# The first two right operands of the up projection's first set, made in a task of the output projection

## Chip, cores and metric

The kernel runs on one core of one Trainium2 chip. The metric is the device time of one execution in microseconds; the time before is the median of three runs. One more execution was taken by the hardware profiler, and all views below come from it.

## What is computed

One decoder layer on 2048 tokens of width 1024: two groups of gated linear attention between two norms, then an MLP with squared ReLU. Cut to what matters here:

```python
def reference(x, w_in, ..., w_out, pre_mix_norm, post_mix_norm, pre_mlp_norm, post_mlp_norm, w_up, w_down):
    h = x
    mix = hybrid_mixer(rmsnorm(h, pre_mix_norm), w_in, ..., w_out)   # (2048, 1024); ends with "@ w_out"
    h = h + rmsnorm(mix, post_mix_norm)
    u = rmsnorm(h, pre_mlp_norm) @ w_up                              # (1024, 4096)
    m = jnp.square(jax.nn.relu(u)) @ w_down                          # (4096, 1024)
    return h + rmsnorm(m, post_mlp_norm)
```

All inputs and the output are float32.

## The kernel before

**Products of split operands.** Each float32 operand is split in a high part (an ACT copy, rounded to float32r) and a low part (the difference, on DVE or POOL). A product is three matmuls: high by high, high by low, low by high. In `up`'s `product` these are L1064 (high parts), L1065 (left's low part) and L1066 (right's low part).

**Stages.** The mixer runs over four blocks of 512 tokens. Each ends with `out_proj`, which multiplies by w_out in two halves of columns. For each 128 tokens (a row of tokens, in what follows) a `residual` task then scales the result (L867), adds the input (L868), squares it for the next norm (L870 on ACT), stores it to out (L873), scales it again (L874), transposes it on TensorE (L880) and stores it to a scratch tensor. After the mixer comes `up`, then `down`.

**Up as a seven-product scheme.** Each 2 x 2 block product is done with seven products of sums instead of eight. The left operands come from activations: sums that `combine` has stored in h_operands. The right ones come from w_up: for one *set* (256 columns of w_up) four blocks b11, b12, b21, b22, from which `right` makes seven operands, number 0 being b11 itself, number 5 being t2 = b22 - t1 with t1 = b12 - b11, and so on (t4 = b21 - t2). Products go in the order 0, 5, 1, 6, 4, 3, 2; 0 and 1 collect in PSUM bank X, 5, 6 and 3 in Y, 4 and 2 in Z. There are 16 sets for each half of the tokens.

**What overlaps.** For the last block, `out_proj` asks SP to load the first set's raw weights in two stage tiles (`st`, 128 x 1024), long ahead, and starts the task `first_left`. It loads the eight quarters of left operands 0 and 5 from h_operands in `ct` tiles (128 x 512, 15 slots), and splits them (`left`, L934; `parts`, whose ACT copy is L951; `tt`, L948 on DVE or L945 on POOL). The set's right operands are made by `right` in tiles of a pool that lies where the mixer's weights were, so only when the output projection has read those. `up` first runs the products of sets 0 and 1 that can begin within seven slots, among the last `residual` steps (L874 to L884).

**What sets the order.** Tasks are Python generators. `step` advances each by one yield; that gives the order in which instructions are recorded. A scheduler of the framework then orders them, engine by engine, by its own estimate of times, and each engine runs its list in order. SP issues nearly all DMAs, in order too: one that waits holds those behind it. `tt` chooses DVE or POOL by the load it has given each so far.

The second copy of the layer (`exact`) is for inputs outside the range of the fast one and does not run here.

Of the kernel before, what the change touches and what calls it, by code (L numbers as in the profile page):

```python
# [7 lines left out]
F32 = mybir.dt.float32  # L8
F32R = mybir.dt.float32r
I32 = mybir.dt.int32  # L10
AF = mybir.ActivationFunctionType
ALU = mybir.AluOpType
# [4 lines left out]
P = 128  # L17
# [49 lines left out]
class Weights:  # L67
# [17 lines left out]
    def part(self):  # L85
        y = self.layer
        return y.wp.tile([P, 2, WS], F32R, tag="w", name=y.name("w"), bufs=self.LIVE)
# [59 lines left out]
class Layer:  # L147
# [631 lines left out]
    def out_proj(self, b):  # L779
        nc = self.nc  # L780
        mix = [self.t([P, D], "wide") for _ in range(NCH)]
        ss = [self.t([P, 2], "ssm", bufs=8) for _ in range(NCH)]
        heads = [2 * u + h for u in UNITS for h in range(2)]

        def part(z, t, w, ks):
            for i in ks:
                a = tuple(s[:, t * P:(t + 1) * P] for s in self.oT[heads[i]])
                self.mm3(z, a, w[i], i, KT)

        def evac(z, t, half):  # L790
            nc.scalar.activation(mix[t][:, half * 512:half * 512 + 512], z, AF.Copy)
            junk = self.ct()
            nc.scalar.activation(junk, z, AF.Square, accum_out=ss[t][:, half:half + 1])

        if b + 1 < NBLK:
            self.hn[b + 1] = []
            nxt = self.prepare(b + 1)
        else:
            self.ops = {(0, i): [] for i in self.ORDER}
            st = [self.stage(), self.stage()]  # L800
            for x in st:
                self.after(x, self.rs[b][0])
            self.first = [self.up_raw(0, half, x) for half, x in enumerate(st)]
            nxt = self.first_left()
        w, zs = [], []
        for t in range(NCH):
            self.w.pump(2)
            zs.append(self.zp())
            for i in range(6):
                if t == 0:  # L810
                    w.append(self.w.take())
                part(zs[t], t, w, (i,))
                if i % 3 == 2:
                    self.step()
        while len(self.oT) < 8:
            self.step()
        if not self.exact:
            self.spawn(nxt)
        w += [self.w.take(), self.w.take()]
        for t in range(NCH):  # L820
            part(zs[t], t, w, (6, 7))
            if t == NCH - 1:
                self.w.free(KT)
            evac(zs[t], t, 0)
            self.w.pump(2)
            if t % 2:
                self.step()
        w = []
        for t in range(NCH):
            z = self.zp()  # L830
            for i in range(KT):
                if i % 4 == 0:
                    self.w.pump(2)
                if t == 0:
                    w.append(self.w.take())
                part(z, t, w, (i,))
                if t == NCH - 1:
                    self.w.free()
                if i == 3:
                    self.step()  # L840
            evac(z, t, 1)
            self.step()
        for t in range(NCH):
            self.spawn(self.residual(b * TB + t * P, mix[t], ss[t], t))
        if self.exact:
            self.spawn(nxt)
            self.drain()
        elif b + 1 < NBLK:
            self.drain(nxt)
    def first_left(self):  # L850

        for i in self.ORDER[:2]:
            yield from self.left(0, i, self.ct, self.ops[0, i], self.aslots)

# [118 lines left out]
    def up(self):  # L973
# [4 lines left out]
        with ExitStack() as ctx:  # L978
# [3 lines left out]
            def new(tag, n, dt=F32, width=512):  # L982
                sb = upa if tag in ("ev", "a") else self.upw
                return sb.tile([P, width], dt, tag=tag, name=self.name(tag), bufs=n)
# [26 lines left out]
            def right(n):  # L1011

                g = n % NG
                raw = []
                for half in range(2):
                    r = self.up_raw(g, half, new("wr", 4, F32, 1024)) if n else self.first[half]
                    raw += [r[:, :, :P], r[:, :, P:]]
                b11, b12, b21, b22 = raw
                w = sets[n] = {}
                part = lambda z: self.parts(  # L1020
                    *(new("w", 12, F32R).rearrange("p (k n) -> p k n", k=4) for _ in range(2)), z)

                def t():
                    return new("t", 5).rearrange("p (k n) -> p k n", k=4)

                yield
                w[0] = part(b11)
                t1 = t()
                self.tt(t1, b12, b11, ALU.subtract)
                yield  # L1030
                t2 = t()
                self.tt(t2, b22, t1, ALU.subtract)
                w[5] = part(t2)
                yield
                w[1] = part(b21)
                t4 = t()
                self.tt(t4, b21, t2, ALU.subtract)
                yield
                t3 = t()
                self.tt(t3, b22, b12, ALU.subtract)  # L1040
                w[6] = part(t3)
                yield
                w[4] = part(t1)
                yield
                w[3] = part(t4)
                yield
                w[2] = part(b22)
                yield
# [98 lines left out]
            def do(n, what):  # L1147
                if isinstance(what, int):
                    left(n // NG, what)
                    return  # L1150
                if (n, what) not in run:
                    run[n, what] = {
                        "product": lambda: product(n), "right": lambda: right(n),
                        "combine": lambda: self.combine(n // NG + 1, quarters),
                        "down": lambda: self.first_down(new),
                    }[what]()
                next(run[n, what], None)
# [402 lines left out]
```

## Time and profile before

| | |
|---|---|
| three runs | 2253.69 to 2256.93 us, median 2256.26 |
| the profiled execution | 2258.14 us, span of its instructions 2256.3 us |
| TensorE busy | 2201.9 us (98%) |
| DVE, ACT, POOL busy | 1416.8, 1090.1, 643.5 us |
| granted TensorE clock | 0.994 |
| first matmul of up | 982.41 us from the span's start |

PE is TensorE's matmuls, PEld its weight loads, DVE the vector engine, ACT the scalar engine, POOL GpSimd, SP the queue that issues DMAs. In a timeline a row is start, duration, engine, line, operation, what is written <- what is read, and in brackets how long the engine stood before it and who ended the wait. [...] In the table of stretches each engine has its busy time in the stretch. Line numbers in all profile rows are those of the kernel before.

### The profile page before, as it was taken

The numbers are of one execution on the slowest core, as the hardware profiler recorded it, in microseconds if no ns is written. First come the engines' busy times: TensorE is split into PE (matmuls) and PEld (weight loads), VectorE is DVE, ScalarE is ACT, GpSimd is POOL, SyncE is SP. The second block draws the span as 40 slices with busy tenths as digits, with TensorE's granted clock in tenths as the row PEclk, the third lists the DMA queues.
The fourth block names the chain that finished last, engine by engine and source line by source line (L and its number), as shares of the span: only waits on it lengthen the run. The fifth ranks groups of instructions, "written<-read, shape, count | busy, mean of one in ns | idle before, by whom it ended". The sixth has DMA issues, their size and how long they took to land.

```text
span 2256.3 us, 30683 instructions
## 1 busy us (share of the span) xinstructions
PE 2201.9 (98%) x10922; PEld 1830.0 (81%) x10922; DVE 1416.8 (63%) x2273; ACT 1090.1 (48%) x2104; POOL 643.5 (29%) x444
## 2 busy tenths in 40 slices
PE   8999999999999999999999999999999999999996
PEld 7788888888888878876888878888778878888885
DVE  7765566444643475377765686656536876777687
ACT  6664565335543554366555665555542332233255
POOL 4444301010100220035522333223312333232344
PEclk9999999999999999999999999999999999999998
DMA  7766974477536974478744564443534343443357
GB/s 241 259 236 247 330 252 149 159 254 266 184 130 237 352 263 159 144 249 293 279 155 153 183 223 160 154 151 139 196 107 137 125 131 103 131 140 119 115 148 134
DMA packets 249810, 428.02 MB, mean 190 GB/s; under 512 B 19872, under 2 KB 93872, under 8 KB 249648
## 3 DMA queue, kind: packets, MB, share of 16 engines
q1 hardware_dynamic: 245520, 418.10, 54.0%
q0 software_dynamic: 3552, 6.82, 1.9%
q8 instruction: 88, 1.44, 0.3%
q10 hardware_dynamic: 576, 1.05, 0.1%
q14 instruction: 74, 0.61, 0.1%
HBM read 289.44 MB, written 136.45 MB: 189 GB/s over the span
## 4 chain that ended last, share of the span: by engine, by line
PE 49%; DMA 2%; DVE 1%; ACT 1%; issue 1%; POOL 1%; SPq 0%; DVEq 0%; ACTq 0%; POOLq 0%
PE Y_f L1365 4%; PE Y_f L1366 3%; PE Y_f L1367 3%; PE Y_f L1064 3%; PE Y_f L1065 3%; PE Y_f L1066 3%; PE X_f L1365 2%; PE X_f L1367 2%; PE Z_f L1064 2%; PE Z_f L1065 2%; PE X_f L1366 2%; PE Z_f L1066 2%; PE Z_f L1365 2%; PE Z_f L1367 2%; PE X_f L1066 2%; PE Z_f L1366 2%
## 5 line engine op out<-in xcount | busy, mean ns | idle before, releaser
L301 PE MATMUL zp_f<-w_f,act_f 128*128 128x512 f32 (+2 forms) x896 | 328.2, 367 | 4.1 <-DVE ct_f L319 3.3
L302 PE MATMUL zp_f<-w_f,act_f 128*128 128x512 f32 (+2 forms) x896 | 324.5, 362 | 0.0
L303 PE MATMUL zp_f<-w_f,act_f 128*128 128x512 f32 (+2 forms) x896 | 323.1, 363 | 0.0
L951 ACT ACTIVATE u_f<-raw_f 128x1024 fp32r<-128x1024 f32 x107 | 113.9, 1064 | 333.2 <-PE Y_f L1366 220.9
L310 POOL TENSOR_TENSOR rs_f<-ms_f,c_neghalf 128x1 f32<-128x1 f32 (+1 forms) x80 | 65.2, 821 | 651.2 <-DVE ms_f L308 645.6
L945 POOL TENSOR_TENSOR u_f<-raw_f,u_f 128x1024 fp32r<-128x1024 f32 x49 | 119.9, 2448 | 306.6 <-ACT u_f L951 305.6
L301 PEld LDWEIGHTS zp_f<-w_f,act_f 128*128 128x128 f32 x896 | 168.5, 188 | 31.0 <-DVE ct_f L319 3.7
L303 PEld LDWEIGHTS zp_f<-w_f,act_f 128*128 128x128 f32 x896 | 168.8, 188 | 24.6 <-issue 0.5
L302 PEld LDWEIGHTS zp_f<-w_f,act_f 128*128 128x128 f32 x896 | 168.9, 188 | 24.0 <-issue 0.5
L301 PE MATMUL zp_f<-act_f,w_f 128*128 128x512 f32 x384 | 151.9, 399 | 8.1 <-ACT act_f L294 8.1
L302 PE MATMUL zp_f<-act_f,w_f 128*128 128x512 f32 x384 | 152.3, 397 | 0.1
L303 PE MATMUL zp_f<-act_f,w_f 128*128 128x512 f32 x384 | 151.9, 396 | 0.0
L1320 DVE TENSOR_TENSOR acc_f<-acc_f,Y_f 128x1024 f32<-128x1024 f32 (+1 forms) x91 | 107.5, 1182 | 65.5 <-PE Y_f L1367 64.4
L1365 PE MATMUL Y_f<-act_f,u_f 128*128 128x512 f32 x368 | 143.7, 394 | 4.2 <-ACT u_f L951 2.2
L1366 PE MATMUL Y_f<-act_f,u_f 128*128 128x512 f32 x368 | 144.4, 392 | 0.0
L1367 PE MATMUL Y_f<-act_f,u_f 128*128 128x512 f32 x368 | 143.9, 393 | 0.1
L951 ACT ACTIVATE w_f<-t_f 128x512 fp32r<-128x512 f32 x128 | 80.2, 630 | 111.3 <-PE Y_f L1065 56.3
L292 POOL TENSOR_TENSOR w_f<-wr_f,w_f 128x512 fp32r<-128x512 f32 (+1 forms) x76 | 104.5, 1385 | 102.3 <-ACT w_f L291 98.4
L1066 PE MATMUL X_f<-act_f,w_f 128*128 128x512 f32 x256 | 100.8, 394 | 5.4 <-DVE w_f L948 3.8
L1084 DVE TENSOR_TENSOR ev_f<-Y_f,p_f 128x512 f32<-128x512 f32 x94 | 64.6, 687 | 63.1 <-PE Y_f L1066 63.1
L948 DVE TENSOR_TENSOR w_f<-t_f,w_f 128x512 fp32r<-128x512 f32 x96 | 80.2, 836 | 36.7 <-ACT w_f L951 36.7
L1320 DVE TENSOR_TENSOR acc_f<-acc_f,Z_f 128x1024 f32<-128x1024 f32 (+1 forms) x62 | 73.2, 1181 | 47.6 <-PE Z_f L1367 47.4
(302 smaller groups left out, 5773.7 us busy)
## 6 DMA issues: line engine op xcount, KB each, us to landing
w_f<-w_split SPq DMA_DIRECT2D x188, 512.0 KB, 6.2
raw_f<-u_operands SPq DMA_DIRECT2D x224, 256.0 KB, 3.1
u_operands<-ev_f SPq DMA_DIRECT2D x223, 256.0 KB, 2.1
w_split<-w_f SPq DMA_DIRECT2D x64, 512.0 KB, 5.2
wr_f<-in_w_up SPq DMA_DIRECT2D x62, 512.0 KB, 3.5
wide_f<-in_x SPq DMA_DIRECT2D x32, 512.0 KB, 7.0
wr_f<-in_w_mix SPq DMA_DIRECT2D x64, 256.0 KB, 5.0
wr_f<-in_w_down SPq DMA_DIRECT2D x28, 512.0 KB, 4.4
```

Source lines behind the costliest of these rows:

```text
L301: mm(out, a[0], b[0], start=i == 0, stop=False)
L302: mm(out, a[0], b[1], start=False, stop=False)
L303: mm(out, a[1], b[0], start=False, stop=i == n - 1)
L945: nc.gpsimd.tensor_tensor(out, a, b, op)
L951: self.nc.scalar.activation(hi, raw, AF.Copy)
L1064: mm(z, whi[:, k, :], hi, start=first and k == 0, stop=False, skip_group_check=more)
L1065: mm(z, whi[:, k, :], lo, start=False, stop=False, skip_group_check=more)
L1066: mm(z, wlo[:, k, :], hi, start=False, stop=end, skip_group_check=more)
L1320: nc.vector.tensor_add(a[:, cols], a[:, cols], z[:, cols])
L1365: mm(zx, hi[:, k, tok], whi, start=not loaded and k == 0, stop=False, skip_group_check=loaded)
L1366: mm(zx, hi[:, k, tok], wlo, start=False, stop=False, skip_group_check=loaded)
L1367: mm(zx, lo[:, k, tok], whi, start=False, stop=k == 1, skip_group_check=loaded)
```

## The change

`out_proj` of the last block keeps the two stage tiles in `self.raw`. `first_left`, before its loads and splits of the left operands, now makes the first set's right operand 0 (split of b11), the differences t1 and t2, and right operand 5 (split of t2), with a yield after each. They go in six `ct` tiles of the mixer instead of the `w` and `t` tiles of up's pool. `right` takes them from there for set 0 and makes them as before for all others. No load, split or matmul is added or left out.

```diff
@@ out_proj @@
             self.first = [self.up_raw(0, half, x) for half, x in enumerate(st)]
+            self.raw = st
             nxt = self.first_left()
@@ first_left @@
+        b11, b12, _, b22 = (r.rearrange("p (k n) -> p k n", k=4)[:, :, h * P:h * P + P]
+                            for r in self.raw for h in range(2))
+
+        def new(dt=F32):
+            return self.ct(dt).rearrange("p (k n) -> p k n", k=4)
+
+        w0 = self.parts(new(F32R), new(F32R), b11)
+        yield
+        t1 = new()
+        self.tt(t1, b12, b11, ALU.subtract)
+        yield
+        t2 = new()
+        self.tt(t2, b22, t1, ALU.subtract)
+        yield
+        self.first_right = w0, self.parts(new(F32R), new(F32R), t2), t1, t2
+        yield
         for i in self.ORDER[:2]:
             yield from self.left(0, i, self.ct, self.ops[0, i], self.aslots)
@@ right, in up @@
                 yield
-                w[0] = part(b11)
-                t1 = t()
-                self.tt(t1, b12, b11, ALU.subtract)
+                if n:
+                    w[0] = part(b11)
+                    t1 = t()
+                    self.tt(t1, b12, b11, ALU.subtract)
                 yield
-                t2 = t()
-                self.tt(t2, b22, t1, ALU.subtract)
-                w[5] = part(t2)
+                if n:
+                    t2 = t()
+                    self.tt(t2, b22, t1, ALU.subtract)
+                    w[5] = part(t2)
+                else:
+                    w[0], w[5], t1, t2 = self.first_right
                 yield
                 w[1] = part(b21)
```

What this does to the order shows at three places. In the changed kernel the lines behind the added ones have other numbers: L934 is L952, L873 is L891, L862 is L880, L962 is L980; L867, L868, L874 are L885, L886, L892; L880 is L898; L945, L948, L951 are L963, L966, L969; L1064 to L1066 are L1086 to L1088.

SP, around the stores of the first two rows of tokens to out, before (three of the eight ct loads stand above these rows):

```order
L934 DMA ct_f_9413<-h_operands 128x512
L934 DMA ct_f_9431<-h_operands 128x512
L873 DMA out<-wide_f_9164 128x1024
L934 DMA ct_f_9451<-h_operands 128x512
L934 DMA ct_f_9469<-h_operands 128x512
L934 DMA ct_f_9489<-h_operands 128x512
L873 DMA out<-wide_f_9165 128x1024
L962 DMA wr_f_9555<-in_w_up 128x1024
L962 DMA wr_f_9557<-in_w_up 128x1024
```

And now, with all eight:

```order
L952 DMA ct_f_9423<-h_operands 128x512
L891 DMA out<-wide_f_9164 128x1024
L952 DMA ct_f_9443<-h_operands 128x512
L952 DMA ct_f_9461<-h_operands 128x512
L952 DMA ct_f_9481<-h_operands 128x512
L952 DMA ct_f_9499<-h_operands 128x512
L891 DMA out<-wide_f_9165 128x1024
L980 DMA wr_f_9542<-in_w_up 128x1024
L952 DMA ct_f_9519<-h_operands 128x512
L980 DMA wr_f_9544<-in_w_up 128x1024
L952 DMA ct_f_9549<-h_operands 128x512
L952 DMA ct_f_9568<-h_operands 128x512
```

Four quarters of left operands have moved behind the first store, three behind the second, and the last three stand among the loads of set 1's raw weights (wr).

DVE, from the second row's scaling on (act is a split left operand, t and w those of right operands, ms, ss and rs belong to the norms), before:

```order
L874 TENSOR_SCALAR wide_f_9620<-wide_f_9165,rs_f_9663 128x1024
L867 SCALAR_TENSOR_TENSOR wide_f_9166<-wide_f_9166,rs_f_9726,post_f_656 128x1024
L948 TENSOR_TENSOR t_f_9541<-st_f_9172 128x512
L868 TENSOR_TENSOR wide_f_9166<-wide_f_9166,wide_f_9720 128x1024
L948 TENSOR_TENSOR t_f_9543<-st_f_9173,t_f_9541 128x512
L864 TENSOR_TENSOR ss_f_9791<-ssm_f_9171 128x1
L948 TENSOR_TENSOR t_f_9567<-st_f_9173,st_f_9172 128x512
L948 TENSOR_TENSOR t_f_9585<-wr_f_9555 128x512
L308 TENSOR_SCALAR ms_f_9748<-ss_f_9746 128x1
L308 TENSOR_SCALAR ms_f_9793<-ss_f_9791 128x1
L948 TENSOR_TENSOR w_f_9546<-t_f_9543,w_f_9545 128x512
```

And now, from the first of its subtractions behind that scaling on:

```order
L966 TENSOR_TENSOR t_f_9540<-st_f_9173,ct_f_9389 128x512
L966 TENSOR_TENSOR t_f_9559<-st_f_9173,st_f_9172 128x512
L886 TENSOR_TENSOR wide_f_9166<-wide_f_9166,wide_f_9720 128x1024
L966 TENSOR_TENSOR w_f_9537<-st_f_9173,w_f_9536 128x512
L966 TENSOR_TENSOR t_f_9582<-wr_f_9542 128x512
L882 TENSOR_TENSOR ss_f_9791<-ssm_f_9171 128x1
L966 TENSOR_TENSOR t_f_9628<-wr_f_9544,t_f_9582 128x512
L308 TENSOR_SCALAR ms_f_9748<-ss_f_9746 128x1
L308 TENSOR_SCALAR ms_f_9793<-ss_f_9791 128x1
L966 TENSOR_TENSOR t_f_9696<-wr_f_9544,t_f_9628 128x512
L966 TENSOR_TENSOR t_f_9752<-wr_f_9544,wr_f_9542 128x512
L966 TENSOR_TENSOR act_f_9546<-ct_f_9519,act_f_9546 128x512
```

The differences t1 and t2 and the low part of right operand 5 are gone from here, t4 (t_f_9540, on POOL before) is new here, and low parts of left operands follow, which before all stood above.

TensorE, product 5 of set 0 (bank Y_f_9698), before:

```order
L1064 MATMUL Y_f_9698<-act_f_9448,w_f_9545 128x512
L1065 MATMUL Y_f_9698<-act_f_9448,w_f_9545 128x512
L1066 MATMUL Y_f_9698<-act_f_9448,w_f_9546 128x512
L1064 MATMUL Y_f_9698<-act_f_9466,w_f_9545 128x512
L1065 MATMUL Y_f_9698<-act_f_9466,w_f_9545 128x512
L1066 MATMUL Y_f_9698<-act_f_9466,w_f_9546 128x512
```

And now:

```order
L1086 MATMUL Y_f_9698<-act_f_9516,ct_f_9406 128x512
L1087 MATMUL Y_f_9698<-act_f_9516,ct_f_9406 128x512
L1088 MATMUL Y_f_9698<-act_f_9516,ct_f_9407 128x512
L1086 MATMUL Y_f_9698<-act_f_9546,ct_f_9406 128x512
L1086 MATMUL X_f_9948<-act_f_9440,w_f_9578 128x512
L1087 MATMUL X_f_9948<-act_f_9440,w_f_9578 128x512
L1087 MATMUL Y_f_9698<-act_f_9546,ct_f_9406 128x512
L1088 MATMUL Y_f_9698<-act_f_9546,ct_f_9407 128x512
L1086 MATMUL Y_f_9698<-act_f_9565,ct_f_9406 128x512
```

The right operand is a ct tile, and two matmuls of set 1's product 0 (X_f_9948) stand between those of the second quarter, act_f_9546.

## Prediction

> **What bounds the kernel now.** I read the page's list of engines first, then busy time by stretches around the place of the change, then each engine's timeline there.
>
> ```profile
> PE 2201.9 (98%) x10922; PEld 1830.0 (81%) x10922; DVE 1416.8 (63%) x2273; ACT 1090.1 (48%) x2104; POOL 643.5 (29%) x444
> ```
>
> TensorE is busy 2201.9 of 2256.3 us, so every gain has to come out of 54.4 us of idle time. The stretches say where some of it is (columns: stretch, length, then busy us of PE, PEld, DVE, ACT, POOL):
>
> ```profile
> 950.00:980.00 30.00, 30.00 (x135) 24.85 (x134) 13.64 (x23) 15.90 (x35) 3.91 (x6) 1.00 0.69 246
> 980.00:1000.00 20.00, 14.88 (x72) 10.82 (x71) 19.49 (x24) 14.96 (x30) 10.30 (x7) 1.00 0.97 333
> 1000.00:1010.00 10.00, 9.63 (x48) 7.69 (x47) 9.97 (x13) 5.43 (x10) 6.84 (x4) 1.00 0.59 181
> 1010.00:1030.00 20.00, 17.19 (x69) 11.96 (x67) 14.12 (x20) 13.03 (x23) 8.38 (x6) 1.00 0.85 262
> ```
>
> Before 980 TensorE has no idle time and DVE is less than half busy. From 980 to 1010 it is the other way round: DVE works 29.46 of 30 us and TensorE stands 5.49 us. Up's products begin here, and DVE, not TensorE, sets the pace. The TensorE timeline names each wait:
>
> ```profile
> 982.41 0.50 PE L1064 MATMUL X_f<-act_f,w_f 128*128 128x512 f32 x1
> ...
> 984.77 0.50 PE L1066 MATMUL X_f<-act_f,w_f 128*128 128x512 f32 x1 [1.63 <-POOL w_f L945]
> ...
> 988.42 0.50 PE L1066 MATMUL Y_f<-act_f,w_f 128*128 128x512 f32 x1 [0.60 <-DVE w_f L948]
> ...
> 993.70 0.50 PE L1066 MATMUL X_f<-act_f,w_f 128*128 128x512 f32 x1 [0.91 <-DVE w_f L948]
> ...
> 995.39 0.50 PE L1065 MATMUL X_f<-act_f,w_f 128*128 128x512 f32 x1 [0.96 <-DVE act_f L948]
> ...
> 998.93 0.50 PE L1066 MATMUL X_f<-act_f,w_f 128*128 128x512 f32 x1 [0.98 <-DVE w_f L948]
> ...
> 1007.75 1.07 PE L880 MATMUL at_f<-c_ident,wide_f 128*128 128x128 f32 x8 [0.37 <-DVE wide_f L874]
> ...
> 1013.55 0.61 PE L1064 MATMUL Z_f<-a_f,w_f 128*128 128x512 f32 x2
> ...
> 1016.13 0.50 PE L1065 MATMUL Z_f<-a_f,w_f 128*128 128x512 f32 x1 [0.59 <-DVE a_f L948]
> ...
> 1020.03 0.50 PE L1064 MATMUL Y_f<-a_f,w_f 128*128 128x512 f32 x1 [0.60 <-ACT a_f L951]
> ...
> 1030.19 0.50 PE L1064 MATMUL Y_f<-act_f,w_f 128*128 128x512 f32 x1 [1.55 <-DVE ev_f L1084]
> ```
>
> The first two waits, 1.63 + 0.60 = 2.23 us, are for the low parts of the two operands that the change makes earlier. The next four, 0.91 + 0.96 + 0.98 + 0.37 = 3.22, are for other tiles in the same DVE queue. The six make 5.45. Behind them three waits, 0.59 + 0.60 + 1.55 = 2.74, are for operands of the Z and Y products.
>
> **What is removed.** Two stalls, 2.23 us, if the operands are ready; that they will be, DVE and POOL show:
>
> ```profile
> 961.78 1.92 DVE L948 TENSOR_TENSOR act_f<-ct_f,act_f 128x512 fp32r<-128x512 f32 x3 [9.85 <-ACT act_f L951]
> ```
>
> ```profile
> 965.98 0.55 POOL L310 TENSOR_TENSOR rs_f<-ms_f,c_neghalf 128x1 f32<-128x1 f32 x1 [19.88 <-DVE ms_f L308]
> ```
>
> DVE has been idle 9.85 us and POOL 19.88 when the task's new steps (three DVE subtractions, one on POOL, two ACT copies) come. At 1.92 / 3 = 0.64 us a subtraction they take some 3 us out of these 10, and TensorE wants their results at 982.41. With this cover they cost nothing; were it gone, the old 2.23 us would be back.
>
> **What is moved: the left operands.** The same task loads and splits the eight raw quarters of the left operands 0 and 5, and these steps now come four yields later. SP's queue before:
>
> ```profile
> 958.23 1.91 SPq L934 DMA_DIRECT2D ct_f<-h_operands  x2
> 970.14 0.34 SPq L873 DMA_DIRECT2D out<-wide_f  x1
> 970.52 1.79 SPq L934 DMA_DIRECT2D ct_f<-h_operands  x3
> 977.65 0.34 SPq L873 DMA_DIRECT2D out<-wide_f  x1
> 978.09 1.21 SPq L962 DMA_DIRECT2D wr_f<-in_w_up  x2
> ```
>
> And how long the loads from h_operands took to land between 945 and 1000:
>
> ```profile
> DMA to landing us min/median/max: 2.7/5.7/8.6
> ```
>
> SP issues in order, and the store to out waits until DVE has added the residual. Before, five quarters went ahead of the first store (970.14) and three ahead of the second (977.65). In the new order one goes ahead of the first, four ahead of the second, and three (the last of left operand 5) come behind the second and among the loads of set 1's weights. The first of these is issued at about 978.7 and, by the median of these loads, 5.7 us, lands at 984.4.
>
> So work leaves the DVE queue and other work comes into it. Before, the last left subtraction ended at 978.25:
>
> ```profile
> 977.57 0.68 DVE L948 TENSOR_TENSOR act_f<-ct_f,act_f 128x512 fp32r<-128x512 f32 x1
> ...
> 979.74 0.75 DVE L874 TENSOR_SCALAR wide_f<-wide_f,rs_f 128x1024 f32<-128x1024 f32 x1 [0.66 <-POOL rs_f L310]
> 980.57 1.28 DVE L867 SCALAR_TENSOR_TENSOR wide_f<-wide_f,rs_f,post_f 128x1024 f32<-128x1024 f32 x1
> 981.77 0.68 DVE L948 TENSOR_TENSOR t_f<-st_f 128x512 f32<-128x512 f32 x1
> 982.37 1.22 DVE L868 TENSOR_TENSOR wide_f<-wide_f,wide_f 128x1024 f32<-128x1024 f32 x1
> 983.51 1.75 DVE L948 TENSOR_TENSOR t_f<-st_f,t_f 128x512 f32<-128x512 f32 x1
> ...
> 985.86 1.79 DVE L948 TENSOR_TENSOR t_f<-wr_f 128x512 f32<-128x512 f32 x1
> ```
>
> And POOL's:
>
> ```profile
> 982.43 2.28 POOL L945 TENSOR_TENSOR w_f<-st_f,w_f 128x512 fp32r<-128x512 f32 x1 [1.90 <-ACT w_f L951]
> 985.34 1.75 POOL L945 TENSOR_TENSOR t_f<-st_f,t_f 128x512 f32<-128x512 f32 x1 [0.62 <-DVE ss_f L864]
> ...
> 1005.68 1.38 POOL L945 TENSOR_TENSOR act_f<-raw_f,act_f 128x512 fp32r<-128x512 f32 x1
> ```
>
> The count behind that point: DVE loses three subtractions (two differences, one low part) and gains five (four left quarters, and the difference t4, which POOL had at 985.34). From start to start one takes 0.60 us (981.77 to 982.37), so DVE has 2 x 0.60 = 1.20 us more. POOL loses two (982.43, 985.34) and gains one left quarter. What a POOL subtraction costs DVE is seen in the two DVE rows that run beside one: 1.75 and 1.79 us where it is 0.68 otherwise, so 1.07 and 1.11 lost. Taking one away gives back 1.1 at most and nothing at least. DVE's backlog thus changes by +0.1 to +1.2 us. The rows lie near the lower end, but the new order puts POOL's operations elsewhere, so I take the middle, **+0.7 us**. [...]
>
> **The wait that is added.** The second step of product 5 now needs the left quarter loaded behind the second store. Its low part stands in DVE's order behind the residual sum of the third row of tokens and behind four differences of set 1's weights, which need set 1's loads. Its high part stands in ACT's queue behind the square of that sum. The pitch of TensorE's matmuls, and the end of ACT's square of the second row:
>
> ```profile
> 985.11 0.40 PE L1064 MATMUL X_f<-act_f,w_f 128*128 128x512 f32 x1
> 985.35 0.40 PE L1065 MATMUL X_f<-act_f,w_f 128*128 128x512 f32 x1
> ```
>
> ```profile
> 978.65 0.18 ACT L870 ACTIVATION_READ_ACCUMULATOR wide_f<-wide_f 128x1 f32 x1
> ```
>
> The walk: from 979.4 (the fourth quarter's high part, some 0.6 us after ACT's square ends at 978.83), DVE has by the rows above 0.6 for that quarter, 0.7 scale, 1.2 gain, 1.2 for two differences, 1.15 sum, 3.0 for five subtractions, 0.2 for three small operations and 0.7 for the late quarter itself: 988.15, or 990.35 if two POOL subtractions cost it 1.1 each. TensorE is there far sooner: at 0.23 us a matmul from 982.41, twelve of product 0 and three of product 5 end at 985.8; three more can go before the low part is needed. TensorE waits 1.7 to 3.9 us. Both POOL subtractions shown cost DVE that much, so I take a value toward the upper end, 3.2. The old later waits (3.22 in all) shrink, since the next operands then follow in DVE's queue at 0.6 us each while TensorE has some 20 matmuls and 1 us of transposes; between 0 and 2.8 stay, I take half of the old, 1.6. Idle before the Z products: 3.2 + 1.6 = 4.8 instead of 5.45, a gain of 0.65. But TensorE cannot keep it: at Z it waits for what DVE and ACT split (0.59, 0.60), and this queue is 0.7 later. What is behind the waiting matmul on TensorE: the transposes of the third row of tokens and products of set 1, none of which is wanted by anyone but DVE and ACT.
>
> Everything else is the same work: as many matmuls, as many loads. The later products and the down projection keep their order but for a swap or two.
>
> **Sum.** The profiled execution took 2258.14 us (span 2256.3 and 1.8 around it); with 0.7 it would be 2258.8. It lies 1.9 above the median of the runs, 2256.26, so the median becomes **2257.0 us**. Of this kernel 0.2% is 4.5 us, about the least that a measurement tells from no change.
>
> **The rivals.**
> - *The change does what it is for and no wait comes in its place.* For it: the two waits are read off the timeline, and DVE's idle time before 980 is real. Against it: the three late quarters. It needs their loads to land early and DVE to take them at once; then all six waits go, -5.45: 2250.8. Chance 0.11.
> - *Set 1's weight loads block DVE.* In the new order the four differences that need them stand ahead of the late quarters. Their landing between 975 and 1000:
>
> ```profile
> DMA to landing us min/median/max: 5.0/5.9/7.7
> ```
>
>   The second load (two SP issues after 978.09, at about 979.3) lands at 985.2 with this median, and DVE, which comes to it at 985.5 by the fast walk above, does not wait. From a landing time over about 6.2 us it does. At 8.6, the longest landing among the loads around it, it comes at 987.9, 2.4 us late; with the backlog's upper end of 1.2 and the waits of 2.74 at the Z and Y products once more, because their operands come later too, that is +6.3: 2262.6. Against it speaks that 2.2 of the 2.4 are gone if POOL has slowed DVE twice by then. Chance 0.13.
> - *It does nothing for the first product*, because the left operand, not the right, is what it then waits for. The fourth quarter's low part is ready at 980.1, and wanted at 982.41 + 9 x 0.23 = 984.5. It would need a slip of 4.4 us; then the time stays at 2256.3 to 2258. Chance 0.03.
> - The forecast: 0.73.
>
> **How the numbers follow.** Faster by over 0.2% is the first rival alone, 0.11; slower is the second, 0.13; within 0.2% the rest, 0.76. The forecast's own range is 2255 (the 0.65 and some more kept) to 2259 (1.2 and a longer new wait). To leave out no more than 2 in 10 the range reaches toward both rivals: 2251.5 to 2261.5.
>
> **What would show it.** Right: product 0 runs without a gap; a new wait of 1.7 to 3.9 us for act_f stands in the second step of product 5, near 986 to 990; the waits for w_f of 1.63 and 0.60 are gone; DVE stays over 19 of 20 us busy from 980 to 1000, and the first Z matmul comes within 1.5 us of 1013.5. Wrong: TensorE idle under 2.5 us between 980 and 1010 (the first rival), or DVE idle there with a wait for wr_f (the second), or a difference that arises far from this place.

## The result, and the profile after

The changed kernel takes **2259.59 us** (median; 2255.44 to 2262.58) against 2255.93 (2252.06 to 2258.79) of the kernel before on the same chip: a ratio of **1.0014, 95% interval 1.0007 to 1.0020**. It is slower, by some 3.2 us (1.6 to 4.5), which is inside the 0.2% that the prediction called no change. The profiled execution has a span of 2257.4 us. Its list of engines hardly differs from before:

```profile
PE 2201.3 (98%) x10922; PEld 1829.9 (81%) x10922; DVE 1416.7 (63%) x2273; ACT 1088.1 (48%) x2104; POOL 639.9 (28%) x444
```

The stretches around the change (after PE, PEld, DVE, ACT and POOL come the granted clock, the DMA share and GB/s):

```profile
980.00:1000.00 20.00, 16.59 (x68) 12.69 (x67) 20.00 (x26) 14.46 (x29) 8.24 (x7) 0.83 1.02 343
1000.00:1010.00 10.00, 10.00 (x51) 8.20 (x50) 6.33 (x11) 6.19 (x11) 3.36 (x4) 1.00 0.61 209
1010.00:1030.00 20.00, 16.50 (x60) 11.59 (x58) 14.25 (x17) 11.87 (x21) 7.50 (x5) 0.91 0.80 245
```

From 980 to 1000 TensorE is busy longer than before (16.59 against 14.88) and yet runs fewer matmuls (68 against 72), because the clock granted to it is 0.83 where it was 1.00. DVE now has no idle time there at all. The TensorE timeline shows the first product and the waits up to Z:

```profile
981.05 0.48 PE L1086 MATMUL X_f<-act_f,ct_f 128*128 128x512 f32 x1
...
983.66 0.39 PE L1088 MATMUL X_f<-act_f,ct_f 128*128 128x512 f32 x1
...
986.00 0.51 PE L1086 MATMUL Y_f<-act_f,ct_f 128*128 128x512 f32 x1 [1.27 <-ACT act_f L969]
...
989.24 0.80 PE L1087 MATMUL Y_f<-act_f,ct_f 128*128 128x512 f32 x1 [1.99 <-DVE act_f L966]
...
1013.46 0.73 PE L1086 MATMUL Z_f<-a_f,w_f 128*128 128x512 f32 x2 [1.07 <-ACT a_f L969]
```

Product 0 runs through from 981.05 without a gap. Both old waits for w_f are gone, and in product 5 stand two new ones, 1.27 for the high part and 1.99 for the low part of the quarter that is loaded late. The four old waits behind them are gone as well; idle time between the first X and the first Z is 4.49 us (the three rows up to Z make 4.33 of it) where it was 5.44. But Z comes 32.41 us after the first X, and before 31.14 (1013.55 - 982.41). SP's queue, with the store and the loads of the prediction's step:

```profile
969.10 0.34 SPq L891 DMA_DIRECT2D out<-wide_f  x1
969.49 2.25 SPq L952 DMA_DIRECT2D ct_f<-h_operands  x4
976.60 0.34 SPq L891 DMA_DIRECT2D out<-wide_f  x1
977.04 0.38 SPq L980 DMA_DIRECT2D wr_f<-in_w_up  x1
977.47 0.78 SPq L952 DMA_DIRECT2D ct_f<-h_operands  x1
978.30 0.45 SPq L980 DMA_DIRECT2D wr_f<-in_w_up  x1
978.80 1.04 SPq L952 DMA_DIRECT2D ct_f<-h_operands  x2
```

**Where the time went.** Windows of 3.41 us from the new wait on, after:

```profile
985.05:988.46 3.41, 1.24 (x3) 0.48 (x3) 3.41 (x8) 3.41 (x9) 1.33 (x3) 1.00 1.06 336
988.46:991.88 3.42, 2.51 (x7) 1.72 (x8) 3.42 (x5) 2.13 (x5) 1.87 (x2) 0.50 1.05 392
991.88:995.29 3.41, 3.41 (x12) 2.86 (x11) 3.41 (x4) 2.13 (x4) 1.62 (x1) 0.50 1.07 391
```

and the same place before:

```profile
983.40:986.81 3.41, 2.04 (x9) 1.67 (x10) 3.41 (x5) 3.41 (x7) 2.79 (x2) 1.00 1.02 366
986.81:990.22 3.41, 2.81 (x13) 2.00 (x12) 2.97 (x7) 2.98 (x7) 2.08 (x4) 1.00 1.08 397
990.22:993.64 3.42, 2.57 (x16) 1.88 (x14) 3.42 (x4) 2.49 (x5) 2.77 (x2) 1.00 1.08 373
993.64:997.05 3.41, 2.39 (x9) 1.70 (x10) 3.41 (x5) 0.65 (x2) 1.15 (x1) 1.00 0.68 205
```

Before, the idle time is spread: 1.37, 0.60, 0.85 and 1.02 us in four windows, all at full clock. After, 2.17 us stand in one, and for the 6.8 us behind it TensorE is granted half its clock. A later stretch differs as well. 1030 to 1100, first before, then after:

```profile
1030.00:1100.00 70.00, 67.81 (x282) 55.09 (x283) 55.35 (x60) 42.25 (x74) 44.90 (x30) 0.95 0.94 313
```

```profile
1030.00:1100.00 70.00, 65.82 (x284) 52.59 (x285) 54.81 (x58) 41.47 (x72) 45.08 (x30) 1.00 0.89 309
```

TensorE stands 70 - 65.82 = 4.18 us there, before 2.19. Two things weaken this reading. Before's profile has two windows of half clock in that stretch (the mean is 0.95), after's has none. And from the first X to 1100, as a whole, TensorE stands about as long in both: 10.45 us before, 11.09 after. The changed kernel stands later, and less before.

### The profile page after: what moved, and what is told of

Read it like the earlier page. It is cut to its first block, busy times and chain, and to the rows that moved or that the text cites. A ratio compares the mean times of both kernels' runs of the same rounds, so it can differ in the third digit from the quotient of the medians.

```text
span 2257.4 us, 30692 instructions
## 1 busy us (share of the span) xinstructions
PE 2201.3 (98%) x10922; PEld 1829.9 (81%) x10922; DVE 1416.7 (63%) x2273; ACT 1088.1 (48%) x2104; POOL 639.9 (28%) x444
## 4 chain that ended last, share of the span: by engine, by line
PE 86%; DVE 4%; issue 3%; ACT 3%; DMA 2%; POOL 1%; SPq 0%; DVEq 0%; ACTq 0%; POOLq 0%
PE zp_f L301 10%; PE zp_f L302 10%; PE zp_f L303 10%; PE Y_f L1087 4%; PE Y_f L1086 4%; PE Y_f L1088 4%; PE Y_f L1387 4%; PE Y_f L1388 3%; PE Y_f L1389 3%; PE X_f L1387 2%; PE Z_f L1087 2%; PE X_f L1087 2%; PE X_f L1088 2%; PE Z_f L1088 2%; PE X_f L1086 2%
## 5 line engine op out<-in xcount | busy, mean ns | idle before, releaser
L969 ACT ACTIVATE u_f<-raw_f 128x1024 fp32r<-128x1024 f32 x107 | 113.6, 1062 | 329.8 <-PE Y_f L1388 223.0
L963 POOL TENSOR_TENSOR u_f<-raw_f,u_f 128x1024 fp32r<-128x1024 f32 x49 | 119.8, 2445 | 307.4 <-ACT u_f L969 300.8
L969 ACT ACTIVATE w_f<-t_f 128x512 fp32r<-128x512 f32 x126 | 78.8, 628 | 111.9 <-PE Y_f L1087 55.7
L1086 PE MATMUL Z_f<-a_f,w_f 128*128 128x512 f32 x256 | 100.3, 393 | 1.2 <-ACT a_f L969 1.1
L1087 PE MATMUL Z_f<-a_f,w_f 128*128 128x512 f32 x256 | 100.4, 392 | 0.9 <-DVE a_f L966 0.9
```

The lines of the kernel that those rows point to most:

```text
L963: nc.gpsimd.tensor_tensor(out, a, b, op)
L969: self.nc.scalar.activation(hi, raw, AF.Copy)
L1086: mm(z, whi[:, k, :], hi, start=first and k == 0, stop=False, skip_group_check=more)
L1087: mm(z, whi[:, k, :], lo, start=False, stop=False, skip_group_check=more)
```

## The experiments

Two theories stood against each other. **Clock**: the extra time is half clock behind a concentrated wait. **Queue**: DVE's backlog sets when the next operands come, and TensorE's clock does not matter. A third question was whether the late loads (my step on SP) or the early splits make the new wait. "Loss" below is the mean over a kernel's runs of span x (1 - granted clock), and beside it in brackets that of before on the same chip. It is an upper bound of what the clock can cost: matmuls of 128x512 follow each other by 0.43 us at half clock and by 0.23 at full (in after near 994 and 996), and in the profiled executions 4.7 to 6.9 us of it lie behind TensorE's last matmul. The fourth column is the difference of the means to the runs of before beside it, with a standard error of 0.6 to 1.0 us; "by means" refers to it. The last column is from one profiled execution each. Before's median stood at 2255.4 to 2255.9 in all comparisons.

| kernel | median us | ratio to before, 95% | mean less before's, us | loss us (before's) | idle 1030 to 1100, us |
|---|---|---|---|---|---|
| before, once more | 2256.82 | 1.0007, 0.9998 to 1.0016 | +1.4 | 12.7 (11.1) | 2.82 |
| after, once more | 2259.66 | 1.0016, 1.0007 to 1.0025 | +3.6 | 16.6 (12.1) | 4.26 |
| loads late only | 2257.71 | 1.0010, 1.0001 to 1.0019 | +1.9 | 13.7 (11.1) | 3.84 |
| right operands early only | 2254.43 | 0.9996, 0.9986 to 1.0005 | -1.3 | 11.1 (11.1) | 2.27 |
| the same with one yield | 2257.12 | 1.0005, 0.9996 to 1.0014 | +0.7 | 11.5 (12.4) | 3.50 |
| operand 0 only | 2255.18 | 0.9996, 0.9987 to 1.0005 | -0.4 | 11.7 (11.1) | 3.03 |
| loads on ACT's queue | 2255.04 | 0.9992, 0.9983 to 1.0001 | -0.7 | 14.3 (12.1) | 2.49 |
| after, 8 matmuls in the wait | 2258.72 | 1.0011, 0.9999 to 1.0022 | +2.9 | 15.6 (12.1) | 3.10 |
| after, 14 matmuls in the wait | 2256.76 | 1.0008, 0.9999 to 1.0017 | +2.0 | 13.1 (11.2) | 3.74 |
| ACT's queue and 12 matmuls | 2259.67 | 1.0017, 1.0008 to 1.0026 | +3.6 | 12.7 (11.2) | 5.30 |
| right early, 8 matmuls in down | 2254.77 | 0.9998, 0.9989 to 1.0007 | 0.0 | 11.7 (12.1) | 4.59 |
| late low parts on POOL | 2254.98 | 1.0000, 0.9990 to 1.0009 | +0.1 | 14.8 (12.4) | 1.03 |

**Both kernels once more.**

> The kernel before, once more, so that its granted clock is known run by run. The kernel after lost 2257 x (1 - 0.9925) = 17 us to a lowered clock in the mean of its runs, and took 3.4 us more than before. Theory 'clock' (the extra time is lost in pieces of half clock that follow TensorE's new wait): this kernel loses some 14 us, 2 to 3 less than after, and its time without the loss is within 1 us of after's. Theory 'queue' (TensorE stands longer because DVE's queue got longer): the loss is the same within 1 us and the time without it lies 2 to 4 us below after's. Both: a ratio of 1.000 within 0.001.

> The kernel after, once more, on one chip with the three below and with the granted clock of each run. From the runs so far: before loses 2254 x (1 - 0.9951) = 11.1 us to a lowered clock (mean of 33 runs) and takes 2244.4 without the loss, after lost 16.6 and takes 2242.5. Theory 'clock': this repeats, a loss 3 to 6 us over before's and a time without it 1 to 3 us below before's, ratio 1.001 to 1.002. Theory 'queue' (the clock differs between chips, the extra time is DVE's): on one chip the losses are equal within 1 us, and the time without them is 2 to 4 us above before's.

The kernel before stands 1.4 us by means above itself here, so differences of that size in the table are not to be read as effects. The slowdown of after repeats, 1.0016. The loss is 16.6 us in both sets of runs of after and 11.1 to 12.7 in those of before, on one chip 16.6 against 12.1: "clock" is right in its main forecast, that after loses more, though not in all its sizes: before was to lose some 14 us, and lost less. Without the loss the mean of after is 1.0 us below before's on that chip (2242.6 against 2243.6).

What a microsecond of loss is worth can be read from the runs of one kernel on one chip, which differ in nothing but the execution. One more goes with 0.4 us more time among the 118 runs of before beside the experiments, and with 0.6 us among the 25 of after. At that price 4.5 us of loss make some 1.8 to 2.7 us. This is an estimate from a relation between runs, not from a trial.

The second profile has the waits of the first, to 0.01 us, but one window of half clock behind them instead of two:

```profile
980.84 0.48 PE L1086 MATMUL X_f<-act_f,ct_f 128*128 128x512 f32 x1
...
989.03 0.79 PE L1087 MATMUL Y_f<-act_f,ct_f 128*128 128x512 f32 x1 [1.99 <-DVE act_f L966]
...
1011.99 0.73 PE L1086 MATMUL Z_f<-a_f,w_f 128*128 128x512 f32 x2 [1.07 <-ACT a_f L969]
```

Z comes 31.15 us after the first X with one window of half clock, 32.41 with two. So in these two executions of one kernel a second window, half of whose 3.41 us is 1.7, goes with 1.26 us; one window with the new queue makes no difference to before (31.14).

**The two halves of the change apart.** Loads late only, put into the kernel before:

```diff
     def first_left(self):
+        for _ in range(4):
+            yield
         for i in self.ORDER[:2]:
```

> The kernel before with four empty steps ahead of the left operands: their loads slip behind the stores to out just as in the change, and no right operand is made early. Theory 'late quarters' (the slip of the loads is what eats the gain): the two old waits for w_f (1.63 and 0.60) stay, the wait for act_f in the second step of product 5 comes on top, cut by them to 1 to 2 us, and the time is 2 to 5 us above before (2258 to 2261), no better than after. Theory 'right operands' (the early splits themselves cost what they gain, in DVE's queue or elsewhere): the slip is harmless and the time is that of before within 1 us.

Right operands early only, and the same with one yield, are the kernel after with these yields taken out (with one yield, the last of the four stays):

```diff
         w0 = self.parts(new(F32R), new(F32R), b11)
-        yield
         t1 = new()
         self.tt(t1, b12, b11, ALU.subtract)
-        yield
         t2 = new()
         self.tt(t2, b22, t1, ALU.subtract)
-        yield
         self.first_right = w0, self.parts(new(F32R), new(F32R), t2), t1, t2
-        yield
```

> The kernel after with the four yields between the new steps taken out: the right operands are made early in one step, and all eight quarters of the left operands are loaded ahead of the second store to out, as before. Theory 'late quarters': product 5 no longer waits for act_f, or under 1 us; TensorE's idle time between the first product and the first Z falls from 4.5 to 1 to 3 us, and the time is 2 to 5 us under before (2251 to 2254). Theory 'queue': the first wait is gone but the same DVE work stands ahead of the first Z product, which still comes 31 to 32 us after the first product; the time is that of before within 1.5 us.

> The kernel after with one yield behind the new steps instead of four: four left quarters are loaded ahead of the first store to out and four between the stores, none behind the second. It repeats the question of the kernel without yields (2254.4) in another order of the later work. Theory 'late quarters': no wait for act_f over 1 us in product 5, first Z under 30.5 us behind the first product, and the time 2253 to 2255.5, 1.5 us or more under after by the mean. If the gain there came from a lucky order of the later sets and not from the loads: between 2256 and 2260.

Late loads alone give 1.0010, just under the lower end of what "late quarters" expected, with waits at the places that it named, of other sizes. "No better than after" did not come: the median lies 1.9 us under after's, though by means and with their errors the two are not told apart. The waits:

```profile
983.42 0.50 PE L1068 MATMUL X_f<-act_f,w_f 128*128 128x512 f32 x1 [1.27 <-DVE w_f L950]
...
987.62 0.50 PE L1068 MATMUL Y_f<-act_f,w_f 128*128 128x512 f32 x1 [1.19 <-POOL w_f L947]
...
991.07 0.50 PE L1067 MATMUL Y_f<-act_f,w_f 128*128 128x512 f32 x1 [1.11 <-DVE act_f L950]
```

With all eight loads ahead of the second store the wait for act_f in product 5 is gone, and the kernel is back at before's time:

```profile
981.49 0.48 PE L1082 MATMUL X_f<-act_f,ct_f 128*128 128x512 f32 x1
...
988.97 0.50 PE L1084 MATMUL X_f<-act_f,w_f 128*128 128x512 f32 x1 [1.07 <-DVE w_f L962]
...
999.90 0.50 PE L1084 MATMUL X_f<-act_f,w_f 128*128 128x512 f32 x1 [1.32 <-DVE w_f L962]
...
1010.89 0.73 PE L1082 MATMUL Z_f<-a_f,w_f 128*128 128x512 f32 x2 [1.01 <-ACT a_f L965]
```

The first Z comes 29.40 us after the first X, 1.7 sooner than before; of this 1.3 us arrive at the end by means, and the interval of the ratio holds 1. It did not reach the 2 to 5 us that "late quarters" forecast: idle between X and Z is still 3.98, now for other operands in DVE's queue. "Queue" has its time, within 1.5 us of before, but not its first Z, 31 to 32 us after the first X. The kernel with one yield has no wait for act_f over 0.16 us there either, but Z comes after 30.74 us (I had said under 30.5) and the time is 2257.12, outside the 2253 to 2255.5 forecast. It lies in the range of the other branch, by which the kernel without yields owes its gain to a lucky order of the later sets.

So without the slip the change gains nothing that can be measured. With the slip, after takes 4.9 us more by means than without yields and 2.8 more than with one, each measured against before on its own chip and with an error of about 1.0. The halves don't add: late loads +1.9 us by means, early operands -1.3, both together +3.6; each alone is about as much as the kernel before differs from itself, the 4.9 is not.

**Only operand 0 early.**

```diff
+        self.first_right = self.parts(new(F32R), new(F32R), b11)
         for i in self.ORDER[:2]:
...
-                    w[0] = part(b11)
+                w[0] = part(b11) if n else self.first_right
```

> Only the right operand of product 0 is made early, with no yield of its own, and the differences t1, t2 and operand 5 stay in the up stage, in their old place. The loads of the left quarters keep the order of before but for one. Theory 'late quarters': the wait of 1.63 goes and the one of 0.60 stays or grows to 1.5; 0.5 to 2 us under before. Theory 'queue': the time is that of before within 1 us, since the first Z comes as late as it did.

Its time is before's, as "queue" said, and its 0.4 us less is just short of the 0.5 of "late quarters". The first wait is gone, the second is larger, 0.77 + 1.08, and Z comes 31.81 us after X:

```profile
987.24 0.50 PE L1073 MATMUL Y_f<-act_f,w_f 128*128 128x512 f32 x1 [0.77 <-ACT w_f L960]
...
989.06 0.50 PE L1075 MATMUL Y_f<-act_f,w_f 128*128 128x512 f32 x1 [1.08 <-DVE w_f L957]
```

**Loads from ACT's queue.**

```diff
-            self.nc.sync.dma_start(raw, self.hcd[i, s, j])
+            q = self.nc.scalar if raws == self.ct else self.nc.sync
+            q.dma_start(raw, self.hcd[i, s, j])
```

> The kernel after with the loads of the eight left quarters issued from ACT's queue instead of SP's, so that no store to out stands ahead of them; the four yields stay. Theory 'late quarters behind the stores' (my step on SP): the wait for act_f in product 5 goes to under 1 us, and the time to that of the kernel with all eight loads ahead of the store, 2253 to 2256. If instead the yields themselves hold the splits back (the task's place in DVE's and ACT's order, whoever issues the load), the wait stays over 2 us and the time at 2258 to 2261.

The time is the one that the "stores" theory gave, and its reason is wrong: the last three loads are issued even later, behind ACT's own work, and the wait stays.

```profile
980.21 0.84 ACTq L953 DMA_DIRECT2D ct_f<-h_operands  x2
```

```profile
987.95 0.79 PE L1087 MATMUL Y_f<-act_f,ct_f 128*128 128x512 f32 x1 [2.61 <-ACT act_f L970]
...
989.98 0.80 PE L1088 MATMUL Y_f<-act_f,ct_f 128*128 128x512 f32 x1 [0.29 <-DVE act_f L967]
```

A wait of 2.90 us with 6.8 us of half clock behind it, and 2255.04 us all the same. So the wait in product 5 and the half clock do not make the slowdown by themselves. This kernel stands 2.49 us from 1030 to 1100, after 4.18, and from the first X to 1100 it stands 8.67, after 11.09.

**Useless matmuls in the wait.** They change nothing that is computed, since their bank is started afresh behind them. There are 8, 14 or, with the loads on ACT's queue, 12:

```diff
                     whi, wlo = sets[n].pop(i)
+                    for _ in range(8 if n == 0 and i == 5 else 0):
+                        nc.tensor.matmul(z, whi[:, 0, :], ops[s, i][0][0], start=True, stop=False, skip_group_check=True)
```

> The kernel after with 8 useless matmuls (some 8 x 0.23 = 1.8 us) on TensorE ahead of product 5 of set 0, into the bank that this product then starts afresh; the loads and DVE's order around the place stay. The wait for act_f shrinks from 3.3 to about 1.5 us by them, so TensorE stands less and does no more that counts. Theory 'clock': the stretch of half clock behind the wait, 6.8 us in after's profile, is gone from 985 to 1000; the loss falls by 2 to 4 us and the time to 2255 to 2257.5, under after's although TensorE has 8 matmuls more. Theory 'queue': Z comes when DVE has made its operands, 32 us after the first product as in after; the time is after's within 1 us.

> The kernel after with 14 useless matmuls (14 x 0.22 = 3.1 us) ahead of product 5 of set 0, since 8 took up the first of the two waits only and left 2.00 + 0.83 with a piece of half clock behind them. Now the waits at this place should be under 1.5 us together. DVE's order up to there is after's; a few operations of the sets behind it change places. Theory 'clock': no half clock between 985 and 1000, the loss over the run 2 to 4 us below after's 16.6, the time 2255 to 2257.5. Theory 'queue' (DVE's backlog, not TensorE's clock, decides when the next operands come): the first Z product comes 31 to 32.5 us after the first product all the same, and the time is 2258 to 2260.5, that of after.

> The kernel whose left quarters are loaded from ACT's queue (2255.0 us, with a loss to a lowered clock of 14.3 and 2240.6 without it) with 12 useless matmuls (2.7 us) ahead of product 5 of set 0; its profile had a wait of 2.61 + 0.29 there with 6.8 us of half clock behind it. Theory 'clock': that stretch is gone, the loss falls by 1.7 to 3.4, and the time is 2251.5 to 2253.5, below both kernels. Theory 'queue': within 1 us of 2255.

Eight fill only the first of the two waits; 2.00 and 0.83 stay, with a window of half clock behind them, and the result is inconclusive. Fourteen do what was wanted:

```profile
982.46 0.48 PE L1088 MATMUL X_f<-act_f,ct_f 128*128 128x512 f32 x1
...
990.67 0.50 PE L1089 MATMUL Y_f<-act_f,ct_f 128*128 128x512 f32 x1 [0.68 <-DVE act_f L966]
...
992.46 1.06 PE L898 MATMUL at_f<-c_ident,wide_f 128*128 128x128 f32 x8 [0.82 <-DVE wide_f L892]
...
1013.60 0.73 PE L1088 MATMUL Z_f<-a_f,w_f 128*128 128x512 f32 x2 [1.07 <-ACT a_f L969]
```

```profile
985.00:1000.00 15.00, 13.49 (x63) 10.39 (x62) 15.00 (x21) 11.39 (x22) 5.89 (x6) 1.00 1.00 348
```

The clock is 1.00 from 985 to 1000 and the loss over the run falls from 16.6 to 13.1, as "clock" said; against before beside it, which also differs, from +4.5 to +2.0. The median is 2256.76, in "clock"'s range, with more work on TensorE. By means the time falls by 1.6 us (from +3.6 to +2.0), with an error of 1.2: that is not clear of noise. "Queue" was right in its other forecast: Z comes 31.14 us after X, no sooner than with one window of half clock. Nor is the clock the only thing that changed: further on, SP's order is another than after's, and one wait there is 1.34 us instead of 2.01 (the next section follows that wait back). On the kernel with ACT's queue the filling took the half clock away as well (13.19 us busy of 985 to 1000 at clock 1.00) and made it 4.3 us slower by means, against both forecasts. Its later order moved: this row is 1030 to 1100, where it stands 5.30 us.

```profile
1030.00:1100.00 70.00, 64.70 (x275) 51.98 (x274) 50.91 (x59) 41.43 (x73) 41.80 (x30) 0.98 0.90 308
```

**The same filling at another wait**, the 2.26 us at the first Y product of down, in the kernel with the right operands early:

```diff
                     mm = nc.tensor.matmul
+                    for _ in range(8 if n == 0 and i == 5 and x == xs[0] else 0):
+                        mm(zx, self.u[0, 0][0][:, 0, tok], self.wd[0][0][0][0], start=True, stop=False, skip_group_check=True)
```

> The kernel with the right operands made early in one step and all eight loads ahead of the store (2254.4 us), with 8 useless matmuls in the wait of 2.26 us at the first Y product of down, which its profile shows with a piece of half clock of 3.41 us behind it. Nothing else is moved but one load and one copy. Theory 'clock': that wait shrinks to about 0.5 us, the piece behind it is gone, and with it about 3.41 / 2 = 1.7 us: 2252 to 2253.5. If half clock there costs nothing, since DVE or ACT holds TensorE back anyway: within 0.7 us of 2254.4.

The wait is gone, and so is the half clock behind it:

```profile
1621.26 1.98 PE L1382 MATMUL Y_f<-act_f,act_f 128*128 128x512 f32 x8
...
1623.08 0.39 PE L1385 MATMUL Y_f<-act_f,u_f 128*128 128x512 f32 x1
```

The time is not better, 2254.77 against 2254.43, inside the other branch. But this does not weigh the price of half clock. The profile has a window of half clock at 1614.55 instead, behind another wait, and the loss over the runs is 11.7 us where it was 11.1: there was no clock won that could have arrived.

**The late low parts on POOL**, as many operations on each engine as in after:

```diff
-            out.append(self.parts(*pair(), raw))
+            out.append(self.parts(*pair(), raw, pool=raws == self.ct and i == 5 and j > 0))
```

> The kernel after with the low parts of the last three quarters of left operand 5 made on POOL; three subtractions that POOL had (two of set 0's operands 1 and 6, one quarter of operand 1) go to DVE for them, so both have as many as in after. Loads and yields stay. Theory 'place in DVE's queue' (step 4: the late low part stands behind the sum and four differences): POOL is free and makes it 1.4 to 2 us after ACT's copy, which in after ended at 985.85, so the second wait of 1.99 falls under 0.6, the two together to 1.3 to 2 us, no half clock follows, and the time is 2255 to 2257.5. Theory 'loads' (the quarter is simply not there): the wait stays at 3 us or more and the time at 2258.5 to 2260.5.

The time is before's, 1.0000, by means 3.5 us under after, and at the lower end of the forecast (2254.98 against 2255). The mechanism came only in part. The wait of 1.28 for the high part stays, and one window of half clock; the next wait is 1.62, for another tile:

```profile
986.16 0.50 PE L1090 MATMUL Y_f<-act_f,ct_f 128*128 128x512 f32 x1 [1.28 <-ACT act_f L969]
...
989.02 1.94 PE L898 MATMUL at_f<-c_ident,wide_f 128*128 128x128 f32 x8 [1.62 <-DVE wide_f L892]
```

```profile
1030.00:1100.00 70.00, 68.97 (x303) 56.27 (x302) 59.14 (x64) 43.38 (x76) 45.07 (x30) 1.00 0.96 333
```

What changed most is the later stretch: 1.03 us idle, where after has 4.18, and 7.50 from the first X to 1100, where after has 11.09. Three subtractions traded engines and SP's order moved; which of these did it, no run tells. The kernel with that stretch almost free of idle time has lost the whole slowdown. It still takes a loss of 14.8 us, 2.4 more than before beside it: half clock alone does not make the slowdown.

## Why the prediction was right, and where it fell short

The verdict within 0.2% is right and the time is inside the range. The forecast of 2257.0 is 2.6 us too low, and just outside the likeliest case's own range (2255 to 2259).

- **Removed**: right. Product 0 has no gap, and both waits for w_f are gone.
- **Moved**: right. The stores and loads stand in the order forecast. The first late quarter was issued at 977.47, 1.2 us sooner than I said.
- **The wait added**: right in size, 1.27 + 1.99 = 3.26 against 3.2, and in place. I had not seen that it comes in two parts: the high part, behind ACT's square, is late too. Between X and Z 4.49 us are idle, 4.8 predicted, which is partly luck: of the 1.6 us that I left to the old waits 0.16 remain, and 1.07 come before Z, where the sum had none.
- **DVE's backlog, +0.7**: the size can't be told apart. DVE works 20.00 of 20 us where it worked 19.49. Z relative to X moved by 0.0 and +1.27 us in two profiles, and the half clock is in both.
- **The step that failed** is in the sum: "with 0.7 it would be 2258.8". It counted TensorE's idle time and gave every idle microsecond the same price. Two things are missing. One is the half clock behind the wait: the old waits were spread, the new ones lie together. The loss rose by 4.5 us on one chip, some 1.8 to 2.7 us of time by the relation between runs above. With the half clock taken away at this place the time fell by 1.6 us by means, with an error of 1.2. The other is the order of the work behind.
- **"Everything else is the same work"** holds for the amount, and the rest of that step, that the later products keep their order "but for a swap or two", failed: SP's order differs from before's at many places up to 1070. From 1030 to 1100 TensorE stands 4.18 and 4.26 us in the two profiles of after, 2.19 and 2.82 in the two of before. The largest wait there can be followed back, after:

```profile
1046.85 0.50 PE L1086 MATMUL Y_f<-a_f,w_f 128*128 128x512 f32 x1 [2.01 <-DVE ev_f L1106]
```

```profile
1045.50 0.69 DVE L966 TENSOR_TENSOR ev_f<-ev_f,ev_f 128x512 f32<-128x512 f32 x1 [2.01 <-ACT ev_f L1110]
```

```profile
1043.57 0.73 ACT L921 ACTIVATE st_f<-st_f,pre_f 128x512 f32<-128x512 f32 x1 [4.18 <-issue]
```

```profile
1038.83 0.80 SPq L1119 DMA_DIRECT2D u_operands<-ev_f  x2
1039.72 0.40 SPq L920 DMA_DIRECT2D st_f<-h_scratch  x1
```

TensorE waits for DVE, DVE for a step of ACT, and ACT has stood 4.18 us before the scaling of a tile, which is ahead of that step. SP issued this tile's load at 1039.72, behind two stores of sums. Before, a load of st_f stood ahead of these stores:

```profile
1034.05 0.38 SPq L902 DMA_DIRECT2D st_f<-h_scratch  x1
1037.58 0.80 SPq L1097 DMA_DIRECT2D u_operands<-ev_f  x2
1038.42 0.44 SPq L902 DMA_DIRECT2D st_f<-h_scratch  x1
```

So a load slipped behind blocking stores here too (SP had waited 3.6 us for DVE's ev_f before the first of them), far from the place that I looked at. The three profiles with after's order at this place (after, its repeat, 8 matmuls) have waits of 2.01, 2.08 and 1.97; of the two of before one has none there and the other 1.30, 14 matmuls have 1.34 and the late low parts on POOL 0.41, all four with a load ahead. But three others (loads late only, operand 0 only, loads on ACT's queue) have no load directly ahead and no such wait. And from the first X to 1100, as a whole, the two profiles of after stand 11.09 and 11.55 us, those of before 10.45 and 11.69. So the rows tell where that one wait comes from; what it costs at the end is not shown.
- **The rivals**: none came. No load of set 1's weights held DVE (it has no idle time from 980 to 1000), and the first product was helped. A rival of the right kind, that the same idle time costs more when it lies together, was missing.

**What stays open.** The 3.2 us are not divided to the tenth between the half clock and the later waits: each kernel that takes one away also moves the other. In the table the idle time from 1030 to 1100 goes with the time in many rows, but the kernel filled in down has 4.59 us of it at before's time, and 8 matmuls 3.10 at after's; it is one profile each, and a sign, not a proof. Nor is it shown where in the run the rest of the 4.5 us of loss lies, since only profiled executions tell the place of a slow piece, and there are two each of before and after and one of every other. No version was found that beats the kernel before by more than its interval; the nearest is the one with its loads on ACT's queue, 0.9992.

## What to carry to other kernels

Where one engine feeds another just in time, moving a step earlier moves everything that shares its task and its queues: list what now goes behind the next blocking store, and what that holds back (here three loads behind the store of 976.60, and 3.26 us of wait), before counting the stall that is removed. Price TensorE's idle time by how it lies, not by its sum: 2.17 us within one window brought half clock, 3.84 us spread over four brought none. And when the feeding engine is the bound, do not count on a removed stall or a recovered clock to arrive whole at the end; here a microsecond of loss went with 0.4 to 0.6 us of time among the runs of one kernel.

## What the hardware showed that was not expected

Within the kernel the granted clock falls to half (0.50 in the rows above) in pieces of 3.41 us or a multiple (but for the last piece of each execution, which goes on past TensorE's last matmul: 12.06 us in before, 11.47 in after), and all pieces of one execution lie on one grid of that pitch, whose phase differs from run to run (two pieces start at 1031.18 and 1061.90 in before, 9 times 3.41 us apart, and two at 988.46 and 1015.77 in after, 8 times). I laid this grid over the idle time of TensorE in the 14 profiled executions (between 60 us and 2235 us, leaving out windows at half clock). All 42 windows with 1.95 us idle or more were followed by a window at half clock. So were 12 of the 32 between 1.65 and 1.95, and none of the 8791 below; in the profiles of before and after alone these are 7 of 7, 3 of 6 and none of 1249. A window at half clock was followed by another where it held 0.6 us idle or more (all 7; the one in after held 0.91), and in no other case. So the same wait of about 2 us can be followed by half clock or not, according to where it falls on the grid: the one for ev_f ahead of down's first product, 1.98 us with the right operands early, was followed by none, and that of 1.97 in the kernel filled in down by one piece, from 1614.55. By my estimate this is part of why the runs of one kernel spread over 7 us: time and loss go together with a correlation of 0.44 among the runs of before and 0.79 among those of after.
